# Gated DeltaNet and windowed attention on one core: the merges of the forward and the backward chunk traced in step, their 64x64 products queued in turn

## The chip, the cores and the metric

The program runs on one core of a Trainium2 chip. The metric is the device time of one execution in microseconds (us), as the median of several runs; lower is better. Five engines matter: TensorE (PE; its weight loads are PEld), VectorE (DVE), ScalarE (ACT), GpSimd (POOL), and SyncE (SP), which queues most DMAs. Each engine works through its own queue in the order that was written down when the kernel was built. Line numbers such as L999 are lines of the kernel before.

## The reference: what is computed

One transformer layer over 2048 latent tokens with 256 context tokens in front, model width 1024. Two token mixers run side by side from one input projection:

- A is a bidirectional gated DeltaNet with 4 heads of width 128. It runs over 18 chunks of 128 tokens, once from the front (direction d = 0) and once from the back (d = 1). Inside a chunk the recurrence needs the inverse of a unit triangular matrix of 128x128 for each head; between chunks a 128x128 state of each head is carried on.
- B is windowed attention of 8 query heads over 2 key heads, in blocks of 128 tokens.

Both are gated, projected to width 1024, weighted by sigmoid gates and added, and go through an output projection:

```
y  = sigmoid(ga) * (ya @ w_proj_a) + sigmoid(gb) * (yb @ w_proj_b)
x  = x + gate * (y @ w_out)
```

The inverse in question is `triangular_solve(a_mat, eye)`. A 128x128 triangular matrix with 64x64 diagonal blocks A, B and lower block C has the inverse with blocks A', B' on the diagonal and -B' C A' below, where A', B' are the inverses of the diagonal blocks.

## The kernel before, in words

The program has five parts in time. Up to about 630 us the inputs are normalised and the q, k, v and attention projections are made. From 631 us `gates` makes the 24 row groups of the gate projections in four column groups, 96 tiles in all, by `fm_dense` (L526, L527, L528: one 128x512 product each, 24 products to a tile; their output is called `rps`). VectorE meanwhile inverts the 64x64 diagonal blocks (`base`, L749 and L751; `base4` for the last two chunks, L781 to L793). From about 920 us `scan` runs the two recurrences over 18 steps; then `attention` works through 32 units (a block of 128 queries and one key head); among its later units and after them `project` does the branch projections (L1201 to L1203, output `pps`), and the output projection ends the program.

In a step of the scan each direction has a `chain` (L1055) that carries the state: products `ksps` (L1070), `vps` (L1076) and `sps` (L1088), with VectorE work between them. A `merge` (L969) of each direction makes the whole inverse of the next chunk out of the two 64x64 inverses:

1. two DMAs bring the diagonal blocks into `X` (`mx`), one brings the lower block into `off` (`moff`);
2. TensorE transposes (L988 for d = 0, L990 for d = 1) into the PSUM tile `mtp`;
3. d = 0: ScalarE copies to `W` (L997), four products `myp` (L999), VectorE scales them (L1000), four products `mep` (L1002), ScalarE writes the block (L1003). d = 1: VectorE scales (L1005), four products `myp` (L1007), ScalarE copies (L1008), four products `mep` (L1010), ScalarE writes the block (L1011).

Each of these products is 64 rows by 64 columns in float32, one for each head. The start partition of the operands (0 or 64) picks the half of the rows of PE's 128x128 array, the start partition of the output the half of its columns: so each product works in one quarter of the array. `myp` of d = 0 has rows 64 to 127 and columns 0 to 63, and `myp` of d = 1 has the same quarter. `mep` of d = 0 has rows and columns 0 to 63, `mep` of d = 1 rows 0 to 63 and columns 64 to 127.

The three PSUM tiles of a direction (`mtp`, `myp`, `mep`) take turns in one bank, `mg0` or `mg1`.

The order of the instructions on each engine isn't written by hand. The framework plays the program through a cost model when it is built, and queues what it deems ready, by priority: the scan has high priority, the gate tiles of two column groups (`hh_148` and `hh_150`) fill the gaps that it leaves on TensorE. `tc.issue_after(i)` makes an instruction queue only behind instruction i.

Of the kernel before, what the change touches and what calls it, by code (L numbers as in the profile page):

```python
# [20 lines left out]
H = 4  # L21
# [19 lines left out]
def _hybrid(ctx, tc, nc, V, S, G, T, ins, out, dbg, upto):  # L41
    dma = nc.sync.dma_start
# [17 lines left out]
    ident = cst.tile([128, 128], F32, name="ident")  # L60
# [38 lines left out]
    offsp = [dscr(f"offsp{d}", [NC, 64, H, 64]) for d in range(2)]  # L99
# [3 lines left out]
    Xsp = [{}, {}]  # L103
    X4sp = dscr("X4sp", [2, 2, 4, 8, 64, 16])
# [147 lines left out]
    if True:  # L252
# [48 lines left out]
        for j in range(2):  # L301
            mps = [psum("acc" if n == 0 else "hps", [4, 512], name=f"mps{n}") for n in range(2)]
            for k in range(KT):
# [17 lines left out]
            mtp = psum("kt", [128, 8, 2], name="mtp")  # L321
# [69 lines left out]
        def qk_norm_rope(pool, bufs, ps, nh, c, wn):  # L391
# [28 lines left out]
        def state_pair(c, pss):  # L420
# [64 lines left out]
        for gi in range(8):  # L485
            xts = []
            for j in range(2):
                c = NCB + gi * 2 + j
# [9 lines left out]
            c = NCB + gi * 2  # L498
# [12 lines left out]
    br = pers2.tile([128, NC, 8], F32, name="br")  # L511
# [196 lines left out]
    bs_ = tc.tile_pool(name="base", bufs=1, side="right", reuse_waits="tile")  # L708
# [57 lines left out]
    def base4(fr, bk):  # L766
# [15 lines left out]
        V.tensor_tensor(N[0:32], N[0:32], nb[0:32].unsqueeze(2).to_broadcast(sh), op=ALU.mult)  # L782
        G.memset(X, 0.0)
        for q in range(4):
            if q:
                dma(N[q * 32:q * 32 + 32], N[0:32])
            G.memset(X[q * 32:q * 32 + 32].rearrange("p r s -> p (r s)")[:, 16 * q:16 * q + 976:65], 1.0)
        for m in range(63):
            r, n = 63 - m, m // 4 + 1
            tv = tmp[:, :r * n].rearrange("p (r s) -> p r s", s=n)  # L790
            V.tensor_tensor(tv, N[:, m + 1:, m].unsqueeze(2).to_broadcast([128, r, n]),
                            X[:, m, 0:n].unsqueeze(1).to_broadcast([128, r, n]), op=ALU.mult)
            V.tensor_tensor(X[:, m + 1:, 0:n], X[:, m + 1:, 0:n], tv, op=ALU.add)  # L793
# [47 lines left out]
    LAST = (LAT(14, 15), LAT(0, 1))  # L841
# [35 lines left out]
    def attention(pool, big, blocks, cc):  # L877
        kc, vc, sk, band = cc

        def queries(n):  # L880

            lo_b, hi_b = max(n - 1, 0), min(n + 1, NB - 1)
            nw_ = hi_b - lo_b + 1
            W = nw_ * 128
            t0 = (NCB + lo_b) * 128
# [9 lines left out]
        def scores(n, kv, qq):  # L895
            kw, vw, qT, nw_ = qq
            W = nw_ * 128
            p = big.tile([128, 4, 640], F32, name="pr", bufs=3)
# [67 lines left out]
            weighted(n, kv, qs[n], pr.pop(i))  # L966


    def merge(pool, d, c):  # L969

        X = pool.tile([128, H, 128], F32, name=f"mx{d}", bufs=2)
        G.memset(X, 0.0)
        if c in LAST[d]:
            x4 = pool.tile([128, 4, H, 16], F32, name="x4")
            for b in range(2):
                bs_ = slice(b * 64, b * 64 + 64)
                for q in range(4):
                    dma(x4[bs_, q], X4sp[d, LAST[d].index(c), q, b::2].rearrange("h r s -> r h s"))
                G.tensor_copy(X[bs_, :, bs_].rearrange("p h (s q) -> p h s q", q=4), x4[bs_].rearrange("p q h s -> p h s q"))
        else:  # L980
            for b in range(2):
                dma(X[b * 64:b * 64 + 64, :, b * 64:b * 64 + 64], Xsp[d][c][:, b].rearrange("h r c -> r h c"))
        off = pool.tile([128, H, 64], F32, name=f"moff{d}", bufs=2)
        dma(off[64:128], offsp[d][c])
        tps = psum(f"mg{d}", [128, H, 128], name="mtp")
        for h in range(H):
            if d == 0:
                T.transpose(tps[:, h], X[:, h], ident)  # L988
            else:
                T.transpose(tps[:, h, 64:128], X[64:128, h], ident[64:128, 64:128])  # L990
        brb = br[:, c, d * 4:d * 4 + 4].unsqueeze(2).to_broadcast([128, H, 64])
        y1 = off if d == 0 else pool.tile([128, H, 64], F32, name=f"my{d}")
        yps = psum(f"mg{d}", [128, H, 128], name="myp")
        eps_ = psum(f"mg{d}", [128, H, 128], name="mep")
        if d == 0:
            W = pool.tile([128, H, 128], F32, name="mw", bufs=2)
            S.copy(W, tps)  # L997
            for h in range(H):
                T.matmul(yps[0:64, h, 0:64], lhsT=off[64:128, h], rhs=W[64:128, h, 64:128], start=True, stop=True)  # L999
            V.tensor_tensor(y1[0:64], yps[0:64, :, 0:64], brb[0:64], op=ALU.mult)  # L1000
            for h in range(H):
                T.matmul(eps_[0:64, h, 0:64], lhsT=X[0:64, h, 0:64], rhs=y1[0:64, h], start=True, stop=True)  # L1002
            S.activation(W[0:64, :, 64:128], eps_[0:64, :, 0:64], AF.Copy, scale=-1.0)  # L1003
            return W
        V.tensor_tensor(y1[64:128], tps[64:128, :, 64:128], brb[64:128], op=ALU.mult)  # L1005
        for h in range(H):
            T.matmul(yps[0:64, h, 0:64], lhsT=off[64:128, h], rhs=y1[64:128, h], start=True, stop=True)  # L1007
        S.copy(y1[0:64], yps[0:64, :, 0:64])  # L1008
        for h in range(H):
            T.matmul(eps_[64:128, h, 0:64], lhsT=y1[0:64, h], rhs=X[0:64, h, 0:64], start=True, stop=True)  # L1010
        S.activation(X[64:128, :, 0:64], eps_[64:128, :, 0:64], AF.Copy, scale=-1.0)  # L1011
        return X

    def scan_consts(pool):
        gw = pool.tile([128, 1], F32, name="gw")
# [29 lines left out]
    def scan(pool, pool2, cs):  # L1045

        state = [None, None]
        orders = ([0, 1] + LAT(*range(NB)), [1, 0] + LAT(*range(NB - 1, -1, -1)))
# [50 lines left out]
        def output(d, st, S0, v2):  # L1099
# [26 lines left out]
            else:  # L1126
                dma(osp[b], oa.rearrange("p h d -> p (h d)"))
                seen.add(b)

        W = [merge(pool, d, orders[d][0]) for d in range(2)]  # L1130
        for st in range(NC):
            r = [chain(d, st, W[d]) for d in range(2)]
            ready = [finalize(pool2, b, oa, cs, d) for b, oa, d in late]
            late.clear()
            if st + 1 < NC:
                W = [merge(pool, d, orders[d][st + 1]) for d in range(2)]
            for rest in ready:
                rest()
            for d in range(2):
                if orders[d][st] >= NCB:  # L1140
                    output(d, st, *r[d])
# [3 lines left out]
    with tc.tile_pool(name="scan", bufs=1, side="right", reuse_waits="tile") as scp:  # L1145
        scl_ = tc.tile_pool(name="scan2", bufs=1, reuse_waits="tile")
        scl = scl_.__enter__()
        cs = scan_consts(scl)
# [93 lines left out]
    with tc.tile_pool(name="p4r", bufs=2, side="right", reuse_waits="tile") as pr4, \  # L1242
# [15 lines left out]
        with tc.high_priority(tc.cur_priority - p_last):  # L1258
            yy = load_half(0)
            for k in range(KT):  # L1260
                if k < NWO:
                    pool = pr4 if k < 2 else p4
# [15 lines left out]
        for i, hb in enumerate(halves):  # L1278
# [14 lines left out]
            for tb, n, ps in tiles:  # L1293
                products(tb, n, ps, range(NWO if i == 0 else 0, KT))
                b = hb * 2 + tb
# [56 lines left out]
```

## Time and profile before

| | |
|---|---|
| median of 3 runs | 2039.22 us (2037.51 to 2040.39) |
| the profiled execution, its own time | 2041.74 us |
| span of its trace | 2040.0 us |
| TensorE busy | 1963.6 us, 96% |
| VectorE, ScalarE, GpSimd busy | 1408.4, 786.9, 686.4 us |
| granted TensorE clock, mean | 0.988 |
| first and last product of the merges | 929.1 and 1308.3 us |

The profile lists start and duration of each instruction, and for idle time what ended it. A TensorE record of a matmul lasts longer than the time until the next can start, because they are pipelined; so what a matmul costs TensorE is read from start to start. A float32 product of two float32 operands leaves two records, each with its own weight load: the 72 products of one merge line (18 steps, 4 heads) are 144 records.

### The profile page before, as it was taken

Reading aid. Unit: us, or ns where it says so; the run is one execution under the profiler, and the core shown is the slowest. Engines: PE = TensorE matmul, PEld = TensorE weight load, DVE = VectorE, ACT = ScalarE, POOL = GpSimd, SP = SyncE. Lnnn points to the kernel's source line nnn. Section 1 sums busy time; section 2 is a strip of 40 time slices with the busy share of each in tenths; the row PEclk is TensorE's granted clock in tenths of the full one; section 3 lists DMA queues with packets and bytes.
Section 4 is the critical chain, followed back from the end, with each engine's and each line's share of the span. In section 5 each row is a group of like instructions: output and inputs, shape, how many; then the busy total and the mean of one; then the engine's idle time right before and its main releaser. Section 6 shows DMA issues by size and latency. Waiting matters only on the chain. (4 is left out here: it accounts for less than half of the span.)

```text
span 2040.0 us, 32043 instructions
## 1 busy us (share of the span) xinstructions
PE 1963.6 (96%) x11043; PEld 1641.5 (80%) x11043; DVE 1408.4 (69%) x2715; ACT 786.9 (39%) x1975; POOL 686.4 (34%) x828
## 2 busy tenths in 40 slices
PE   6999999989999899999899999999989999999999
PEld 3888888778898778788788888878868888878887
DVE  6888766667666999999599655636587778743322
ACT  5655555444443322111122222325475556531100
POOL 2862211235652211014222234323256443432321
PEclk7999999999999999999999999999999999999999
DMA  7462236755447533537966788663356655355542
GB/s 254 142 168 81 93 94 166 183 151 158 145 141 195 161 110 112 140 98 222 217 207 205 222 233 226 180 199 123 128 161 204 192 158 169 113 179 180 185 145 93
DMA packets 375510, 333.11 MB, mean 163 GB/s; under 512 B 83832, under 2 KB 299184, under 8 KB 374708
## 3 DMA queue, kind: packets, MB, share of 16 engines
q1 hardware_dynamic: 347924, 288.59, 48.9%
q10 hardware_dynamic: 27424, 42.48, 5.8%
q8 instruction: 87, 1.43, 0.3%
q14 instruction: 75, 0.61, 0.1%
HBM read 220.28 MB, written 109.13 MB: 161 GB/s over the span
## 5 line engine op out<-in xcount | busy, mean ns | idle before, releaser
L526 PE MATMUL rps<-hh,wh 128*128 128x512 f32 x768 | 308.6, 402 | 7.8 <-DVE rt L814 5.6
L528 PE MATMUL rps<-hh,wl 128*128 128x512 f32 x768 | 309.4, 403 | 0.0
L527 PE MATMUL rps<-hl,wh 128*128 128x512 f32 x768 | 307.4, 400 | 0.0
L526 PEld LDWEIGHTS rps<-hh,wh 128*128 128x128 f32 x768 | 145.3, 189 | 43.0 <-DVE rt L814 6.5
L526 PE MATMUL lps<-hh,wh 128*128 128x512 f32 (+1 forms) x448 | 172.1, 384 | 0.3 <-ACT y L636 0.3
L527 PEld LDWEIGHTS rps<-hl,wh 128*128 128x128 f32 x768 | 145.2, 189 | 33.1
L528 PEld LDWEIGHTS rps<-hh,wl 128*128 128x128 f32 x768 | 145.1, 189 | 32.5
L527 PE MATMUL lps<-hl,wh 128*128 128x512 f32 (+1 forms) x448 | 171.1, 382 | 0.0
L528 PE MATMUL lps<-hh,wl 128*128 128x512 f32 (+1 forms) x448 | 171.0, 382 | 0.0
L565 DVE SCALAR_TENSOR_TENSOR cacc<-y,cw,cacc 128x512 f32<-128x512 f32 (+1 forms) x224 | 160.2, 738 | 14.9 <-ACT cacc L563 12.0
L912 DVE CUSTOM_DVE_ANT_0 pr<-sc,band,sk 128x640 f32<-128x640 f32 (+1 forms) x128 | 106.3, 862 | 43.5 <-PE sc L908 22.1
L938 ACT CAST ph<-pt 128x512 fp32r<-128x512 f32 x156 | 90.1, 585 | 111.4 <-PE pt L936 78.9
L940 DVE TENSOR_TENSOR pl<-pt,ph 128x512 fp32r<-128x512 f32 x156 | 104.8, 684 | 39.8 <-ACT ph L938 39.2
L812 ACT ACTIVATE rt<-rps 128x512 f32<-128x512 f32 x96 | 57.2, 596 | 183.2 <-PE rps L528 177.6
L922 POOL TENSOR_SCALAR pr<-pr,sm 128x640 f32<-128x640 f32 (+1 forms) x128 | 98.8, 791 | 56.9 <-DVE sm L920 44.4
L749 DVE TENSOR_TENSOR btmp<-N 128x62 f32<-128x62 f32 (+30 forms) x124 | 115.5, 931 | 3.2
L751 DVE TENSOR_TENSOR N<-N,btmp 128x62 f32<-128x62 f32 (+30 forms) x124 | 114.9, 926 | 3.1
L914 ACT ACTIVATE pr<-pr,sm 128x640 f32<-128x640 f32 (+1 forms) x128 | 104.0, 815 | 24.7 <-DVE sm L912 24.7
L1201 PE MATMUL pps<-yh,wph 128*128 128x512 f32 x256 | 105.5, 416 | 7.2 <-ACT yh L1183 4.1
L245 POOL TENSOR_SCALAR wh<-wr 128x512 fp32r<-128x512 f32 x72 | 48.7, 690 | 172.9 <-PE lps L527 85.3
L246 DVE TENSOR_TENSOR wl<-wr,wh 128x512 fp32r<-128x512 f32 x120 | 91.6, 780 | 20.0 <-POOL wh L245 16.7
L1202 PE MATMUL pps<-yl,wph 128*128 128x512 f32 x256 | 102.2, 399 | 0.5 <-DVE yl L1184 0.5
(302 smaller groups left out, 4950.0 us busy)
## 6 DMA issues: line engine op xcount, KB each, us to landing
wr<-in_w_in_dram SPq DMA_DIRECT2D x120, 256.0 KB
kw<-Ksp SPq DMA_DIRECT2D x28, 384.0 KB
x<-vsp SPq DMA_DIRECT2D x36, 256.0 KB
k<-ksp SPq DMA_DIRECT2D x34, 256.0 KB
kT<-kTsp SPq DMA_DIRECT2D x34, 256.0 KB
wm<-in_w_mod_dram SPq DMA_DIRECT2D x16, 512.0 KB
xt<-in_x_dram SPq DMA_DIRECT2D x16, 512.0 KB
dtl<-Dsp SPq DMA_DIRECT2D x32, 256.0 KB
```

The costliest lines, as they stand in the source:

```text
L526: T.matmul(ps, lhsT=wh[:, k], rhs=xh[:, k], start=k == 0, stop=False)
L527: T.matmul(ps, lhsT=wh[:, k], rhs=xl[:, k], start=False, stop=False)
L528: T.matmul(ps, lhsT=wl[:, k], rhs=xh[:, k], start=False, stop=k == kt - 1)
L565: V.scalar_tensor_tensor(a, y[:, t:t + n], cw[:, m, t:t + 1], a, op0=ALU.mult, op1=ALU.add)
L749: V.tensor_tensor(tv, A[:, m + 1:, m].unsqueeze(2).to_broadcast([h1 + n, r, m]), A[:, m, 0:m].unsqueeze(1).to_broadcast([h1 + n, r, m]), o ...
L751: V.tensor_tensor(A[:, m + 1:, 0:m], A[:, m + 1:, 0:m], tv, op=ALU.add)
L912: V.tensor_tensor_reduce(s_, ps[:, o:768], band[:, b0:b0 + W + 256], -0.125, sk[:, 1, hd:hd + 1], ALU.add, ALU.min, sm[:, h, 1:2])
L914: S.activation(s_, s_, AF.Exp, scale=-1.0, bias=sm[:, h, 1:2], accum_out=sm[:, h, 2:3])
L922: G.tensor_scalar(p[:, h, :W + 256], p[:, h, :W + 256], sm[:, h, 3:4], 1.0, op0=ALU.mult, op1=ALU.mult)
L940: V.tensor_tensor(pl, pt, f32(ph), op=ALU.subtract)
L1201: T.matmul(ps, lhsT=wh[:, k, ms], rhs=hs[k], start=k == 0, stop=False)
L1202: T.matmul(ps, lhsT=wh[:, k, ms], rhs=ls[k], start=False, stop=False)
```

## The change

`merge` now takes both chunks of a step. It loads for both directions first, then transposes for both, then does the two scalings and copies, and then calls `in_step` twice: once for the eight `myp` products, once for the eight `mep` products. `in_step` queues them head by head, forward and backward in turn. The backward `myp` is written to partitions 64 to 127 instead of 0 to 63, which puts it into the quarter with rows and columns 64 to 127; ScalarE's copy behind it reads there and still writes partitions 0 to 63. Sizes, counts of instructions, tiles and PSUM banks are as before.

```diff
-    def merge(pool, d, c):
...
+    def in_step(products):
+        first = None
         for h in range(H):
+            for p in products:
+                with tc.issue_after(first.ins) if first else nullcontext():
+                    i = p(h)
+                first = i
+
+    def merge(pool, cs):
...
+        W, X = pool.tile([128, H, 128], F32, name="mw", bufs=2), Xs[1]
+        S.copy(W, tp[0])
+        V.tensor_tensor(y1[64:128], tp[1][64:128, :, 64:128], brb[1][64:128], op=ALU.mult)
+        yps = [psum(f"mg{d}", [128, H, 128], name="myp") for d in range(2)]
+        in_step([lambda h: T.matmul(yps[0][0:64, h, 0:64], lhsT=offs[0][64:128, h], rhs=W[64:128, h, 64:128],
+                                    start=True, stop=True),
+                 lambda h: T.matmul(yps[1][64:128, h, 0:64], lhsT=offs[1][64:128, h], rhs=y1[64:128, h],
+                                    start=True, stop=True)])
+        V.tensor_tensor(y0[0:64], yps[0][0:64, :, 0:64], brb[0][0:64], op=ALU.mult)
+        S.copy(y1[0:64], yps[1][64:128, :, 0:64])
+        eps_ = [psum(f"mg{d}", [128, H, 128], name="mep") for d in range(2)]
+        in_step([lambda h: T.matmul(eps_[0][0:64, h, 0:64], lhsT=Xs[0][0:64, h, 0:64], rhs=y0[0:64, h],
+                                    start=True, stop=True),
+                 lambda h: T.matmul(eps_[1][64:128, h, 0:64], lhsT=y1[0:64, h], rhs=X[0:64, h, 0:64],
+                                    start=True, stop=True)])
+        S.activation(W[0:64, :, 64:128], eps_[0][0:64, :, 0:64], AF.Copy, scale=-1.0)
+        S.activation(X[64:128, :, 0:64], eps_[1][64:128, :, 0:64], AF.Copy, scale=-1.0)
+        return W, X
...
-        W = [merge(pool, d, orders[d][0]) for d in range(2)]
+        W = merge(pool, [orders[d][0] for d in range(2)])
...
-                W = [merge(pool, d, orders[d][st + 1]) for d in range(2)]
+                W = merge(pool, [orders[d][st + 1] for d in range(2)])
```

In the changed kernel `myp` stands at L1016 and L1018, `mep` at L1023 and L1025; lines behind `merge` are 17 higher.

TensorE at the second merge of the scan, where the forward and the backward `myp` stood apart. Before:

```order
L1088 MATMUL sps<-v_10230,k_10220 128x128 x4
L999 MATMUL myp<-mw,moff_10262 64x64 x4
L1088 MATMUL sps<-v_10249,k_10239 128x128 x4
...
L526 MATMUL rps<-hh_148,wh 128x512
L527 MATMUL rps<-hl_149,wh 128x512
L528 MATMUL rps<-hh_148,wl 128x512
L1007 MATMUL myp<-my_10294,moff_10287 64x64 x4
L528 MATMUL rps<-hh_150,wl 128x512
```

The same place now:

```order
L1016 MATMUL myp<-mw,moff_10262 64x64
L1105 MATMUL sps<-v_10249,k_10239 128x128 x4
L1018 MATMUL myp<-my_10280,moff_10268 64x64
L1016 MATMUL myp<-mw,moff_10262 64x64
L1018 MATMUL myp<-my_10280,moff_10268 64x64
L1016 MATMUL myp<-mw,moff_10262 64x64
L1018 MATMUL myp<-my_10280,moff_10268 64x64
L1016 MATMUL myp<-mw,moff_10262 64x64
L1018 MATMUL myp<-my_10280,moff_10268 64x64
```

Two groups of four have become one group of seven, with one product left alone in front of it. Over the whole scan the products of the merges stand in 78 unbroken groups before and in 53 now; of the 53, 24 hold all eight products, and 11 hold one.

TensorE among the attention units, where the first products of `project` are queued. Before:

```order
L943 MATMUL av<-pl,vc 128x512
L936 MATMUL pt<-ident,pr 128x128 x4
L1201 MATMUL pps<-yh,wph 128x512
L942 MATMUL av<-ph,vc 128x512
L905 MATMUL sc<-kw,qT 128x384
```

Now:

```order
L936 MATMUL pt<-ident,pr 128x128 x4
L1218 MATMUL pps<-yh,wph 128x512
L1219 MATMUL pps<-yl,wph 128x512
L1220 MATMUL pps<-yh,wpl 128x512
L1218 MATMUL pps<-yh,wph 128x512
L1219 MATMUL pps<-yl,wph 128x512
L1220 MATMUL pps<-yh,wpl 128x512
```

These rows follow from a shift ahead of them. Of the 2304 gate products, 1968 stood ahead of the scan's last transposes (L1040) before, and 2064 do now: 96 have moved into the scan. The gate products ended within the seventh unit of the attention, and end within the fifth now; those of `project` began within the tenth, and begin within the ninth now. From the end of the seventeenth unit on the counts of both agree again.

More of the change, by code (lines that the diff above doesn't have):

```diff
@@ L966, in attention @@
             weighted(n, kv, qs[n], pr.pop(i))
-    def merge(pool, d, c):
[L971 to L985, printed above, removed]
-        for h in range(H):
-            if d == 0:
-                T.transpose(tps[:, h], X[:, h], ident)
-            else:
[L990 to L1012, printed above, removed]
@@ new lines, in in_step @@
+    def in_step(products):
+        first = None
+        for h in range(H):
+            for p in products:
[3 more added lines that the diff above has]
+    def merge(pool, cs):
+        hs = range(H)
+        Xs, offs, tp = [], [], []
+        for d, c in enumerate(cs):
+            X = pool.tile([128, H, 128], F32, name=f"mx{d}", bufs=2)
+            G.memset(X, 0.0)
+            if c in LAST[d]:
+                x4 = pool.tile([128, 4, H, 16], F32, name="x4")
+                for b in range(2):
+                    bs_ = slice(b * 64, b * 64 + 64)
+                    for q in range(4):
+                        dma(x4[bs_, q], X4sp[d, LAST[d].index(c), q, b::2].rearrange("h r s -> r h s"))
+                    G.tensor_copy(X[bs_, :, bs_].rearrange("p h (s q) -> p h s q", q=4),
+                                  x4[bs_].rearrange("p q h s -> p h s q"))
+            else:
+                for b in range(2):
+                    dma(X[b * 64:b * 64 + 64, :, b * 64:b * 64 + 64], Xsp[d][c][:, b].rearrange("h r c -> r h c"))
+            off = pool.tile([128, H, 64], F32, name=f"moff{d}", bufs=2)
+            dma(off[64:128], offsp[d][c])
+            Xs.append(X)
+            offs.append(off)
+        for d in range(2):
+            tps = psum(f"mg{d}", [128, H, 128], name="mtp")
+            for h in hs:
+                if d == 0:
+                    T.transpose(tps[:, h], Xs[0][:, h], ident)
+                else:
+                    T.transpose(tps[:, h, 64:128], Xs[1][64:128, h], ident[64:128, 64:128])
+            tp.append(tps)
+        brb = [br[:, c, d * 4:d * 4 + 4].unsqueeze(2).to_broadcast([128, H, 64]) for d, c in enumerate(cs)]
+        y0, y1 = offs[0], pool.tile([128, H, 64], F32, name="my1")
+        W, X = pool.tile([128, H, 128], F32, name="mw", bufs=2), Xs[1]
[16 more added lines that the diff above has]
+        return W, X
```

## The prediction

> **What bounds the kernel now.** I read the page first, for the engine that is full, then the scan's stretch by windows and waits, since all that the change touches lies there.
>
> ```profile
> span 2040.0 us, 32043 instructions
> PE 1963.6 (96%) x11043; PEld 1641.5 (80%) x11043; DVE 1408.4 (69%) x2715; ACT 786.9 (39%) x1975; POOL 686.4 (34%) x828
> 920.00:1357.00 437.00, 426.46 (x2938) 367.42 (x2938) 299.64 (x699) 107.73 (x361) 140.23 (x215) 0.99 0.74 212
> PE aps L1111 <- DVE oa L1123: 5.1, 2, 4.6
> PE ksps L1070 <- DVE S L1094: 2.4, 1, 2.4
> PE rps L526 <- POOL wh L245: 1.2, 1, 1.2
> PE mtp L990 <- ACT mw L997: 0.7, 1, 0.7
> ```
>
> The windows row has PE, PEld, DVE, ACT and POOL in this order, then clock, DMA share and GB/s; the last four rows are the longest waits of TensorE in the same 437 us. TensorE is busy for 426.5 of them and idle for 10.5, and of that idle time only 0.7 us hangs on a merge. So the scan's stretch is bound by TensorE's own sequence: gate products fill whatever the recurrence leaves. What shortens that sequence shortens the stretch, as long as the moved work is covered.
>
> **What the 64x64 products cost TensorE.** Three places of the trace, TensorE in order of time (start, duration, line, operand, shape, count); what counts is start to start.
>
> ```profile
> 928.79 0.40 PE L527 MATMUL rps<-hl,wh 128*128 128x512 f32 x1
> 929.11 0.68 PE L999 MATMUL myp<-mw,moff 64*64 64x64 f32 x8
> 929.63 0.63 PE L1007 MATMUL myp<-my,moff 64*64 64x64 f32 x8
> 930.19 0.49 PE L528 MATMUL rps<-hh,wl 128*128 128x512 f32 x1
> 930.52 0.40 PE L526 MATMUL rps<-hh,wh 128*128 128x512 f32 x1
> 930.75 0.39 PE L527 MATMUL rps<-hl,wh 128*128 128x512 f32 x1
> ...
> 944.27 1.05 PE L1088 MATMUL sps<-v,k 128*128 128x128 f32 x8
> 945.25 0.68 PE L999 MATMUL myp<-mw,moff 64*64 64x64 f32 x8
> 945.86 1.16 PE L1088 MATMUL sps<-v,k 128*128 128x128 f32 x8
> ```
>
> A gate product normally takes 0.23 us to the next (930.52 to 930.75). A group of eight records alone lasts from 945.25 to 945.86, 0.61 us. To it come the way in and out: 928.79 to 929.11 is 0.32 us where 0.23 is normal, 0.09 more, and 930.19 to 930.52 is 0.33, 0.10 more. So a lone group costs 0.61 + 0.09 + 0.10 = 0.80 us. Two groups behind one another in the same quarter, as here, cost 930.52 - 928.79 - 2 x 0.233 = 1.26 us: the second adds only its records, 0.46 us or 0.058 each. A lone group's 0.80 is thus 8 x 0.058 = 0.47 for the records and 0.33 for entering and leaving.
>
> Two groups in different quarters:
>
> ```profile
> 934.72 0.39 PE L526 MATMUL rps<-hh,wh 128*128 128x512 f32 x1
> 935.04 0.50 PE L1002 MATMUL mep<-moff,mx 64*64 64x64 f32 x5
> 935.33 0.27 PE L1010 MATMUL mep<-mx,my 64*64 64x64 f32 x1
> 935.38 0.22 PE L1002 MATMUL mep<-moff,mx 64*64 64x64 f32 x1
> 935.44 0.22 PE L1010 MATMUL mep<-mx,my 64*64 64x64 f32 x1
> 935.44 0.22 PE L1002 MATMUL mep<-moff,mx 64*64 64x64 f32 x1
> ...
> 935.55 0.45 PE L1010 MATMUL mep<-mx,my 64*64 64x64 f32 x5
> 935.93 0.50 PE L527 MATMUL rps<-hl,wh 128*128 128x512 f32 x1
> 936.27 0.39 PE L528 MATMUL rps<-hh,wl 128*128 128x512 f32 x1
> ...
> 1171.17 0.27 PE L1002 MATMUL mep<-moff,mx 64*64 64x64 f32 x1
> 1171.18 0.27 PE L1007 MATMUL myp<-my,moff 64*64 64x64 f32 x1
> 1171.27 0.22 PE L1002 MATMUL mep<-moff,mx 64*64 64x64 f32 x1
> 1171.29 0.22 PE L1007 MATMUL myp<-my,moff 64*64 64x64 f32 x1
> ...
> 1171.40 0.45 PE L1007 MATMUL myp<-my,moff 64*64 64x64 f32 x5
> 1171.79 0.50 PE L527 MATMUL rps<-hl,wh 128*128 128x512 f32 x1
> ```
>
> At 935 us the backward group starts while three records of the forward one are still to come, and then both run at once, each at 0.058 us. The whole pair costs 936.27 - 934.72 - 0.47 = 1.08 us. The second group starts when the first has about four records left. At 1171 us it is tighter: four records of L1002 were the rest of a group, eight of L1007 followed, and the second stream started 0.01 us behind the first; all twelve took 1171.17 to 1171.79, 0.62 us, what eight alone take. So the riders in the other quarter were free. The change queues the two streams two records by two, so that four records of lead always suffice: I take 0.82 us for a full pair.
>
> Here a rule of the Trainium skill speaks against the change. "TensorE: Matmul & The Clock Gate", Part 3, The mechanism, says that weight loads run beside matmuls in flight only where the row group differs, and that matmuls start and end strictly in program order. Both streams of each new pair share their rows (64 to 127 for `myp`, 0 to 63 for `mep`), so by that rule nothing would overlap. The pair at 935 us shares rows 0 to 63 and does overlap, out of program order; so I go by the rows. What it would make of the time is the second rival.
>
> **The change, term by term.** The products: 576 records stand in 78 groups before. 78 x 0.33 = 25.7 us for entering and leaving, 576 x 0.058 = 33.4 us for records, less about 0.18 us (1.26 - 1.08) in each of some 11 groups that overlap already, 2.0 us: 57 us. Now there are 53 groups, 17.5 us; in them the longer of the two streams sums to 312 records, 18.1 us, and the second streams start 0.01 us late, 0.5 us: 36 us. That saves 21 us of TensorE. If no two streams overlapped, it would be 17.5 + 33.4 = 51, and save 6. The transposes of L990 are also 64 rows; they stand in 21 groups before and 18 now, but 7 shared their entry with a merge group and none does now: I cost that at nothing, within 2 us either way.
>
> Gate products that change place: 96 moved from behind the scan into it, 96 x 0.233 = 22.4 us of TensorE. So the scan ends at 22.4 - 21 = 1.4 us later, with the same cover of each step, and the saving shows only where the gate products are now missing, among the attention units.
>
> ```profile
> 1444.00:1481.00 37.00, 37.00 (x197) 31.13 (x197) 20.43 (x44) 18.34 (x40) 8.82 (x10) 1.00 0.35 111
> 1481.00:1540.00 59.00, 50.16 (x262) 38.38 (x261) 48.91 (x100) 43.61 (x94) 34.23 (x34) 0.97 0.55 168
> 1640.00:1700.00 60.00, 60.00 (x327) 50.68 (x326) 42.80 (x90) 30.62 (x66) 26.85 (x29) 1.00 0.46 144
> ...
> 1481.00:1540.00 59.00, 19.60 (x50) 9.13 (x50) 3.13 (x6) 2.91 (x5) 0.97 0.55 168
> 1540.00:1611.00 71.00, 15.80 (x49) 8.59 (x50) 3.27 (x5) 2.34 (x4) 1.00 0.61 195
> 1481.00:1540.00 59.00, 8.38 (x24) 4.06 (x24) 0.67 (x1) 0.97 0.55 168
> 1540.00:1611.00 71.00, 42.56 (x168) 30.62 (x168) 10.25 (x15) 1.00 0.61 195
> 1640.00:1700.00 60.00, 30.31 (x120) 21.65 (x119) 6.82 (x10) 1.00 0.46 144
> ```
>
> Three rows of all instructions, then two of the tile `av` (ten products to a unit), then three of `pps`. Between 1481 and 1540 us there are five units (50 `av`) with hardly any fill, 11.8 us each, and TensorE is not full: this stretch the vector engines set. Between 1540 and 1611 us five units with 168 fillers take 71 us; 168 x 0.233 = 39.1, so a unit's own work is 6.4 us. Between 1640 and 1700 us 120 fillers in 60 us leave TensorE full at 13.0 us a unit. Now the bare stretch is units five to nine instead of seven to eleven: still five units, 59 us. Behind it, units ten to sixteen have about 25 `pps` products each, as at 1640 us: 7 x 13 = 91 us. Units five to sixteen then take 150 us, where they took 167 (1444 to 1611, to the nearest unit); unit seventeen has 12 products fewer, 2.8 us. Together 20 us come back there, of the 22.4 that left.
>
> Sum: + 1.4 us to the scan's end, - 20 after it, is - 18.6, on the profiled 2041.74 us 2023.1. That execution was 2.5 us above the median 2039.22, so for the median **2021 us**, 0.9% faster.
>
> The waits that the change adds: the forward products now wait for the backward's scaling too, and the other way round. The gate products behind them on TensorE would then stand, and behind those the scan. The cover is long:
>
> ```profile
> L1008 ACT COPY my<-myp x18: 350/364/368, 930.3 to 1298.4; 64x256 f32<-64x256 f32 x18
> ```
>
> The first copy ends at 930.7 us, and its products start at 935.33: 4.6 us of other products lie between, and in the new order about as many gate products stand there. I cost the joint wait at nothing; without that cover it would be up to the 1.2 us of the longest wait on GpSimd above, in each of 36 places.
>
> **The rivals.** *The attention keeps part of it.* The five bare units may become six or seven if the first `pps` products wait for their inputs. For: between 1481 and 1540 us each unit took 11.8 us against 6.4 of own work, so a bare unit more costs up to 5.4 us. Against: the new order puts `project` a unit earlier as well. Two units more, 10.8 us: 2032.
>
> *No overlap in turn.* The pairs in the trace came as blocks, none came two by two; if the alternation broke the overlap, 6 us are saved on TensorE instead of 21. The scan then ends 16.4 us later, the attention returns 20: 2039.2 - 3.6 = 2035.6. Against it speak the records at 1171 us, which alternate singly.
>
> *Slower: the joint queueing makes TensorE wait.* Place: the 36 groups at L1016/L1018 and L1023/L1025. It decides from 18.6 / 36 = 0.52 us a group; at 1.2 us each it is 36 x 1.2 - 18.6 = +25, 2064. For: VectorE once held the scan for 4.6 us (L1123 above) with its queue stuck, and a late scaling of one direction now holds both. Against: 0.7 us in all on merge inputs before, and the cover above.
>
> **How the numbers follow.** Forecast 0.62, attention keeps part 0.16, no overlap 0.13, slower 0.09. The forecast's own range is 2012 to 2028: below it, 22.4 us come back whole and the early idle of TensorE shrinks by some of its 10.5 us; above, half of a bare unit and some new waits. With the second case and most of the third the range is 2012 to 2037. What a measurement can tell is 0.2%, 4 us: faster below 2035.1. Forecast and attention case are faster, of the third a sixth: 0.80; same 0.11; slower 0.09.
>
> **What would show it.** Right: `myp` and `mep` groups alternate at about 0.03 us a record, a full pair from entry to exit near 0.82 us; TensorE's time in 64x64 groups falls by about 21 us; the scan ends within 5 us of before; the stretch from the scan's end to the seventeenth unit is about 20 us shorter. Wrong: alternate records at 0.058 us each; waits of TensorE at L1016 to L1025 of more than a few us in sum; a bare attention stretch of seven units.

## The result, and the profile after

The changed kernel takes 2027.62 us (median of 4 runs, 2026.05 to 2031.62) against 2038.64 us for the kernel before on the same chip (4 runs, 2037.51 to 2040.39): a ratio of 0.9950, 95% interval 0.9936 to 0.9964. So it is faster by 0.5%, 11.0 us. The forecast was 2021 us, a gain of 18 to 19 us: the sign is right, the time lies 0.4 us inside the upper end of the forecast's own range (2012 to 2028), and 7 to 8 us of the gain are missing.

The profiled execution of the change took 2031.62 us, the slowest of its four, 10.1 us less than that of before, where the sum had 18.6; so 8.5 us are missing in this pair. The head and the PE row of its page, the windows row of the same 437 us that the prediction showed, and TensorE's longest waits in it:

```profile
span 2029.9 us, 32046 instructions
PE 1946.6 (96%) x11043; PEld 1629.4 (80%) x11043; DVE 1403.5 (69%) x2715; ACT 786.6 (39%) x1975; POOL 686.3 (34%) x828
...
920.00:1357.00 437.00, 423.12 (x2998) 364.06 (x2997) 301.85 (x700) 110.58 (x362) 138.24 (x212) 0.98 0.74 212
```

```profile
PE ksps L1087 <- DVE S L1111: 7.0, 3, 5.6
PE aps L1128 <- DVE oa L1140: 2.5, 1, 2.5
PE sps L1105 <- DVE v L1096: 1.7, 2, 1.4
PE ops L1139 <- DVE oa L1133: 1.7, 1, 1.7
```

TensorE did 60 records more in the stretch (2998 against 2938) and was busy for less of it: it is idle for 13.9 us instead of 10.5, and its mean clock is 0.98 instead of 0.99. No product of the merges (L1016 to L1025) is in the list of TensorE's waits: the joint input wait didn't come. What grew are waits of the recurrence, all on VectorE: S, oa and v.

TensorE's timeline shows one pair in turn, two of its eight doublets and what stands around it:

```profile
935.72 0.39 PE L527 MATMUL rps<-hl,wh 128*128 128x512 f32 x1
936.04 0.27 PE L1023 MATMUL mep<-moff,mx 64*64 64x64 f32 x1
936.05 0.27 PE L1025 MATMUL mep<-mx,my 64*64 64x64 f32 x1
...
936.50 0.22 PE L1023 MATMUL mep<-moff,mx 64*64 64x64 f32 x1
936.51 0.22 PE L1025 MATMUL mep<-mx,my 64*64 64x64 f32 x1
936.65 0.51 PE L528 MATMUL rps<-hh,wl 128*128 128x512 f32 x1
937.00 0.40 PE L526 MATMUL rps<-hh,wh 128*128 128x512 f32 x1
```

The two streams run 0.01 us apart, each at 0.058 us a record. The pair costs 937.00 - 935.72 - 0.47 = 0.81 us; the forecast had 0.82.

The ends of the scan are its first transpose and its last `fps`, here from the views of those two lines, before and after:

```profile
L988 PE MATMUL mtp<-ident,mx x72: 271/273/328, 923.1 to 1297.6; 128*128 128x128 f32 x72
L1040 PE MATMUL fps<-ident,oa x64: 270/273/332, 1191.3 to 1351.5; 128*128 128x128 f32 x64
```

```profile
L1006 PE MATMUL mtp<-ident,mx x72: 270/272/273, 924.3 to 1302.3; 128*128 128x128 f32 x72
L1057 PE MATMUL fps<-ident,oa x64: 270/272/299, 1195.6 to 1361.3; 128*128 128x128 f32 x64
```

The scan took 428.4 us and takes 437.0, so it ends 9.8 us later, not 1.4; 1.2 of that is a later start, whose cause no run here isolates. From its end to the last `pps` the profile before has 506.4 us, now 486.5: 19.9 us come back.

**The scan, term by term.** All tables below are made in the same way, from the records of TensorE between the first `mtp` and the last `fps`: gate products at 0.233 us each; the merges as start-to-start time in their groups with the way in and out; idle time of TensorE as the stretch less its busy time; and the time lost to the clock, as the sum of (1 - granted clock) over windows of 10 us.

| in us | before | change | difference | forecast |
|---|---|---|---|---|
| merges | 57.0 | 36.8 | -20.2 | -21 |
| gate products (775, 871) | 180.6 | 202.9 | +22.4 | +22.4 |
| TensorE idle | 10.2 | 13.9 | +3.7 | 0 |
| lost to the clock | 5.1 | 8.5 | +3.4 | 0 |
| the scan, as measured | 428.4 | 437.0 | +8.6 | +1.4 |

The four terms make +9.3 where +8.6 was measured. The 0.7 us between them is counted twice: a half clock costs nothing while TensorE stands idle, and of the clock's losses 1.45 us in the change and 0.79 before fall into waits.

### The profile page after: what moved, and what is told of

It reads as the page before. It is cut to its first block, busy times and chain, and to the rows that moved or that the text cites. A ratio compares the mean times of both kernels' runs of the same rounds, so it can differ in the third digit from the quotient of the medians.

```text
span 2029.9 us, 32046 instructions
## 1 busy us (share of the span) xinstructions
PE 1946.6 (96%) x11043; PEld 1629.4 (80%) x11043; DVE 1403.5 (69%) x2715; ACT 786.6 (39%) x1975; POOL 686.3 (34%) x828
## 5 line engine op out<-in xcount | busy, mean ns | idle before, releaser
L565 DVE SCALAR_TENSOR_TENSOR cacc<-y,cw,cacc 128x512 f32<-128x512 f32 (+1 forms) x224 | 159.9, 736 | 14.7 <-ACT cacc L563 11.8
```

Of the source, the lines that this page charges most:

```text
L565: V.scalar_tensor_tensor(a, y[:, t:t + n], cw[:, m, t:t + 1], a, op0=ALU.mult, op1=ALU.add)
```

## The experiments

All runs in one table. Ratios are to the kernel before on the same chip, whose median was 2038 to 2042 us; a kernel's runs spread by some 5 us to either side, so the interval is what counts. The last four columns are of the scan, as above.

| kernel | median, us | ratio, 95% interval | gate products | merges | idle | clock |
|---|---|---|---|---|---|---|
| before | 2038.6 | 1 | 775 | 57.0 | 10.2 | 5.1 |
| the change | 2027.6 | 0.9950 (0.9936 to 0.9964) | 871 | 36.8 | 13.9 | 8.5 |
| the change again | 2030.2 | 0.9953 (0.9937 to 0.9968) | 871 | 36.8 | 12.4 | 6.8 |
| in turn, same quarter | 2037.7 | 0.9987 (0.9974 to 1.0000) | 823 | 49.6 | 10.4 | 3.4 |
| blocks, other quarter | 2042.8 | 1.0009 (0.9994 to 1.0024) | 847 | 46.7 | 14.9 | 6.8 |
| before, quarter alone | 2037.8 | 0.9989 (0.9978 to 1.0000) | 823 | 54.0 | 10.5 | 8.5 |
| change, late base4 | 2024.5 | 0.9916 (0.9899 to 0.9934) | 799 | 35.9 | 11.9 | 5.1 |
| before, late base4 | 2035.3 | 0.9969 (0.9956 to 0.9982) | 775 | 56.0 | 6.1 | 1.7 |
| change, base4 traced later | 2025.7 | 0.9937 (0.9916 to 0.9958) | 799 | 31.8 | 16.1 | 6.8 |
| the same, split on ScalarE | 2035.1 | 0.9970 (0.9958 to 0.9981) | 807 | 34.0 | 17.8 | 6.8 |
| before, no base4 | 2030.5 | 0.9949 (0.9929 to 0.9968) | 727 | 53.9 | 4.4 | 3.4 |
| change, no base4 | 2019.7 | 0.9902 (0.9880 to 0.9925) | 751 | 31.5 | 13.2 | 5.1 |
| before, spill queued by ScalarE | 2041.4 | 1.0004 (0.9989 to 1.0019) | 799 | 54.7 | 9.2 | 3.4 |
| change, spill queued by ScalarE | 2036.0 | 0.9985 (0.9968 to 1.0001) | 847 | 36.5 | 14.5 | 10.2 |

Every edit makes the framework plan the whole order anew, so the count of gate products in the scan moves too; that is why the columns are read, not the medians alone. The columns come from one profiled execution of each kernel. The change has two, and they differ by 1.5 us in idle time and 1.7 in the clock, so differences of that size between two kernels say little.

### What is the gain made of: order, quarter, or both

The same turns, but the backward products go to the forward quarter:

```diff
-                 lambda h: T.matmul(yps[1][64:128, h, 0:64], lhsT=offs[1][64:128, h], rhs=y1[64:128, h],
+                 lambda h: T.matmul(yps[1][0:64, h, 0:64], lhsT=offs[1][64:128, h], rhs=y1[64:128, h],
...
-                 lambda h: T.matmul(eps_[1][64:128, h, 0:64], lhsT=y1[0:64, h], rhs=X[0:64, h, 0:64],
+                 lambda h: T.matmul(eps_[1][0:64, h, 0:64], lhsT=y1[0:64, h], rhs=X[0:64, h, 0:64],
```

> The change with one thing undone: the backward products are written to the same quarter of the array as the forward ones (myp rows 64 to 127, mep rows 0 to 63, columns 0 to 63 both), still queued in turn. Theory A (the time is won by streams that overlap): no record overlaps, the eight products of a pair take 16 x 0.058 us; with the 46 groups of the order that results the merges cost TensorE 46 x 0.33 + 576 x 0.058 = 49 us against 36 in the change and 57 before, so the time lies 10 to 13 us above the change, 2037 to 2041, about where before stood. Theory B (the time is won by queueing the merges together, fewer groups and another order): it stays within 4 us of the change, 2024 to 2032.

Blocks of four in different quarters, instead of turns:

```diff
-        for h in range(H):
-            for p in products:
+        for p in products:
+            for h in range(H):
```

> The change with the alternation undone: four forward products, then four backward ones, in the change's quarters. Theory A: the second stream starts when the first has about four records left, a full pair costs 1.08 instead of 0.82 us; with 55 groups the merges cost about 44 us, 8 more than in the change: 2033 to 2037. Theory B: within 4 us of the change, 2024 to 2032.

The kernel before, with only the backward `myp` moved to the other quarter:

```diff
-            T.matmul(yps[0:64, h, 0:64], lhsT=off[64:128, h], rhs=y1[64:128, h], start=True, stop=True)
-        S.copy(y1[0:64], yps[0:64, :, 0:64])
+            T.matmul(yps[64:128, h, 0:64], lhsT=off[64:128, h], rhs=y1[64:128, h], start=True, stop=True)
+        S.copy(y1[0:64], yps[64:128, :, 0:64])
```

> The kernel before with only the quarter changed: the backward myp goes to partitions 64 to 127; the merges are traced one after the other as before. Theory A: the groups stay mostly apart (69 of them), merge cost about 53 us against 57: 4 us less than before at most, 2033 to 2039. Theory B (fewer groups and another order): the same, since little changes in either. It tells whether the quarter alone is worth anything.

TensorE's timeline at the first `myp` pair, in turn in the same quarter:

```profile
932.01 0.40 PE L527 MATMUL rps<-hl,wh 128*128 128x512 f32 x1
932.34 0.33 PE L1016 MATMUL myp<-mw,moff 64*64 64x64 f32 x2
932.51 0.28 PE L1018 MATMUL myp<-my,moff 64*64 64x64 f32 x2
932.62 0.28 PE L1016 MATMUL myp<-mw,moff 64*64 64x64 f32 x2
...
933.75 0.40 PE L526 MATMUL rps<-hh,wh 128*128 128x512 f32 x1
```

And as blocks in different quarters:

```profile
928.12 0.40 PE L527 MATMUL rps<-hl,wh 128*128 128x512 f32 x1
928.45 0.50 PE L1016 MATMUL myp<-mw,moff 64*64 64x64 f32 x5
928.74 0.27 PE L1018 MATMUL myp<-my,moff 64*64 64x64 f32 x1
...
928.96 0.45 PE L1018 MATMUL myp<-my,moff 64*64 64x64 f32 x5
...
929.68 0.39 PE L526 MATMUL rps<-hh,wh 128*128 128x512 f32 x1
```

In the same quarter each group of two records takes 0.115 us and nothing overlaps: 933.75 - 932.01 - 0.47 = 1.27 us a pair. As blocks the second stream starts when the first has three records left: 929.68 - 928.12 - 0.47 = 1.09 us. In turn and in different quarters it is 0.81. Over the scan that makes 49.6, 46.7 and 36.8 us, from 57.0 before; the quarter alone gives 54.0. So neither half of the change does it: of the 20.2 us, 12.8 hang on the other quarter (49.6 to 36.8); the other 7.4 come with the order, which leaves 46 groups with a way in and out in that kernel where 78 were. This split is rough: in the kernel before, the backward `mep` already had a quarter of its own, and the kernel in turn in the same quarter takes that away too. In time the first and the third of these kernels gain 0.1%, which is at the edge of what their intervals tell from nothing, and the blocks gain nothing: TensorE there waited 6.0 us in one piece for a load of the merge, a wait that no other kernel of this group has at that size:

```profile
PE mtp L1008 <- DMA mx<-Xsp: 6.0, 1, 6.0
```

The blocks' time missed both forecasts, which had counted only the merges; in the scan 72 more gate products (16.8 us), 4.7 us more idle time and 1.7 us of clock stand against the 10.3 us saved.

### Is the missing part the step at 993 us

In the change, the longest wait is the state S of the scan's fourth step. VectorE's timeline there, of the change and then of before:

```profile
993.18 4.41 DVE L781 TENSOR_TENSOR N<-N,btmp 32x4096 f32<-32x4096 f32 x1 [11.58 <-DMA N<-Nsp]
997.52 1.52 DVE L246 TENSOR_TENSOR wl<-wr,wh 128x512 fp32r<-128x512 f32 x1
999.07 0.69 DVE L814 SCALAR_TENSOR_TENSOR rt<-rt,rps 128x512 f32<-128x512 f32 x1
999.67 0.82 DVE L246 TENSOR_TENSOR wl<-wr,wh 128x512 fp32r<-128x512 f32 x1
1000.41 2.14 DVE L1111 SCALAR_TENSOR_TENSOR S<-S,tot,sps 128x128 f32<-128x128 f32 x8
```

```profile
994.37 4.41 DVE L781 TENSOR_TENSOR N<-N,btmp 32x4096 f32<-32x4096 f32 x1 [11.16 <-DMA x<-vsp]
998.72 2.14 DVE L1094 SCALAR_TENSOR_TENSOR S<-S,tot,sps 128x128 f32<-128x128 f32 x8
```

S is queued behind a scaling of `base4` that stands for 11 us and a further 4.4, in both kernels; in the change two `wl` and one `rt` came between as well. I queued L781 later (in the change, and further below in the kernel before):

```diff
-        V.tensor_tensor(N[0:32], N[0:32], nc_.unsqueeze(1).to_broadcast(sh), op=ALU.mult)
+        with tc.issue_after(tiles_done[25].ins):
+            V.tensor_tensor(N[0:32], N[0:32], nc_.unsqueeze(1).to_broadcast(sh), op=ALU.mult)
...
-            V.scalar_tensor_tensor(t, t, 1.0, ps, op0=ALU.add, op1=ALU.mult)
+            tiles_done.append(V.scalar_tensor_tensor(t, t, 1.0, ps, op0=ALU.add, op1=ALU.mult))
...
-    base4(*LAST)
...
-        gates(list(range(4)), (1, 0))
+        gates(list(range(6)), (1, 0))
+        base4(*LAST)
...
-        gates(list(range(4, BESIDE)), (1, 0))
+        gates(list(range(6, BESIDE)), (1, 0))
```

> The change, with the scaling that starts the last inversion (L781) queued later on VectorE, behind the evacuation of a later gate tile, so that VectorE's queue no longer stands 11.6 us for the DMA of N while the state update of the scan waits behind it; base4 and two gate row groups are traced ahead of the scan for that. Theory C (the missing 8 us are stalls at that DMA, whose time does not move with TensorE): the 5.6 us wait of ksps on S and the 2.5 us of aps on oa shrink to under 2 us together and the time falls 5 to 8 us below the change, 2019 to 2023. Rival: the wait turns up elsewhere on VectorE's queue and the time stays within 3 us of the change, 2025 to 2030.

> The change itself, unaltered, beside the next three on one chip, so that they are compared with it and not across chips. Expected from its earlier runs: 2024 to 2032, 8 to 14 us under the kernel before.

The second of these is the changed kernel unaltered, on another chip: 0.9953, so the gain of 0.5% stands. The account of its scan stands in kind: merges 36.8 again, and VectorE keeps TensorE waiting for 12.0 us where it was 12.9. It doesn't stand in size: idle time and clock are 3.9 us over before, not 7.1, in a profiled execution 3.7 us shorter than that of the result. The late base4 gave 0.9916, 2024.46 us, between the two expected spans and the best time of a kernel that does all the work. The wait for S is gone, and others stand in its place:

```profile
PE fps L1058 <- DVE oa L1051: 3.3, 4, 1.8
PE ops L1140 <- DVE oa L1137: 3.2, 1, 3.2
PE ops L1140 <- DVE oa L1134: 1.8, 2, 1.7
```

Next `base4` was only traced later; L781 is queued as the planner likes:

```diff
-    base4(*LAST)
...
+        gates(list(range(6)), (1, 0))
+        base4(*LAST)
...
+        gates(list(range(6, BESIDE)), (1, 0))
```

> The change with base4 traced behind the gate row groups 0 to 5 and not ahead of them; nothing is forced on VectorE's queue (L781 stands at the same place as in the change, so the 11.6 us wait on its DMA should stay). The planner's order differs: 41 merge groups instead of 53 (31 of them whole), 24 gate products moved into the scan instead of 96. Theory A (the time follows what the merges cost TensorE): 41 x 0.33 + 0.058 x 288 + 0.5 = 31 us against 36, so 4 to 6 us below the change, 2020 to 2024. Theory C (stalls at the DMA of N set it): the same stall, so within 3 us of the change, 2025 to 2030.

2025.69 us, at the lower edge of the second span: S still kept TensorE for 5.1 us. Then both kernels without `base4`'s loads of N and its steps on VectorE, which takes L781 out of the question:

```diff
-            dma(N[p0:p0 + 16], Nsp[d][c:c + 2].rearrange("c h b r i -> (c h b) r i"))
-        sh = [32, 64, 64]
-        V.tensor_tensor(N[0:32], N[0:32], nc_.unsqueeze(1).to_broadcast(sh), op=ALU.mult)
...
-        for m in range(63):
...
-            V.tensor_tensor(X[:, m + 1:, 0:n], X[:, m + 1:, 0:n], tv, op=ALU.add)
```

> The kernel before without the work of the last inversion: base4 loads no N, does none of its VectorE steps and writes identity blocks, so the output is not the layer's; everything else is kept. Made as the partner of the next one. 20 to 40 us of VectorE work and a DMA wait of 11 us are gone; TensorE is the bound, so only stalls go: 2026 to 2037.

> The change with the same work left out of base4. In these two orders the merges cost 50 us (67 groups) and 31 us (41 groups), 19 apart. Theory C (the missing 8 us are stalls of VectorE's queue behind base4): without it the change is worth nearly all of that, 15 to 19 us under its partner. Rival (they are lost elsewhere: in the attention, or in other waits of the scan): 8 to 13 us under its partner, as in the full kernels.

The two are 10.7 us apart, as far as the originals (11.0), where the first theory wanted 15 to 19. That theory fell: the missing part doesn't hang on `base4`. Without `base4` in VectorE's queue another instruction stands at the head of it at the same place, and S behind that (VectorE's timeline of the change without `base4`):

```profile
996.13 1.69 DVE L246 TENSOR_TENSOR wl<-wr,wh 128x512 fp32r<-128x512 f32 x2 [10.29 <-POOL wh L245]
997.74 2.15 DVE L1099 SCALAR_TENSOR_TENSOR S<-S,tot,sps 128x128 f32<-128x128 f32 x8
```

### Is it the transfers, or GpSimd in front of VectorE

GpSimd's `wh` in that row stands behind the scaling of `x`, and `x` waits for its load. In the change the load is queued behind a spill of 2 x 1024 KB. I let ScalarE queue the spill, in both kernels, and took the kernel before with the late base4 beside them:

```diff
-            dma(Xset[d][si].rearrange("c h b r j -> (c h b) (r j)"), N[p0:p0 + n].rearrange("p r j -> p (r j)"))
+            (adma if si else dma)(Xset[d][si].rearrange("c h b r j -> (c h b) (r j)"), N[p0:p0 + n].rearrange("p r j -> p (r j)"))
```

> The changed kernel, but the second spill of the finished 64x64 inverses (two transfers of 1024 KB, L761) is queued by ScalarE instead of SyncE. In the changed kernel those two stand at 972.6 us in SyncE's queue, and the x of the scan's fourth step, queued behind them at 986.3, lands at about 993 us; the state S of that step is 5.6 us late for ksps. Theory (the transfers of that step land late, and what TensorE saved in the first steps is waited away there): with the spill in another queue that x starts on GpSimd below 990 us, the wait of ksps for S falls below 2 us, and the scan without its gate products (230 to 234 us in the changed kernel) falls to 227 to 230; 2021 to 2026 us. Rival (the 16 DMA engines are full there, at 0.92 busy, whatever queue asks): x still starts at 992 to 996, the wait stays at 4 to 7 us, 2026 to 2032 us. Gate products queued in the scan: 2040 instead of 2064, 5.6 us less in the scan, which the attention gets.

> The same move of the spill in the kernel before. Theory: its wait of ksps for S in that step is only 2.4 us, so there is less to win: the scan without its gate products goes from 247.6 us to 245 to 248, 2035 to 2040 us; so the difference between this kernel and the changed one with the same move grows from 11 us to 13 to 16. Rival: nothing moves in either, the difference stays at 9 to 12.

> The kernel before, with the late queueing of L781 that took the changed kernel from 0.995 to 0.992 of the time before (base4 traced behind six column groups, its first scaling queued behind the 26th gate tile). Theory (the change overtook the transfers, so the step at 993 us costs the changed kernel more than the kernel before): worth 0 to 2.4 us here, 2036 to 2039 us, with the same 1968 gate products. Rival (the late base4 is worth the same to both): 3 to 6 us, 2033 to 2036.

GpSimd's timeline in the change, and in the change with the spill in the other queue:

```profile
993.81 6.13 POOL L1080 TENSOR_TENSOR x<-x,rin 128x512 f32<-128x512 f32 x2 [8.37 <-DMA x<-vsp]
```

```profile
996.04 6.33 POOL L1080 TENSOR_TENSOR x<-x,rin 128x512 f32<-128x512 f32 x2 [7.36 <-DMA x<-vsp]
```

The `x` starts at 996.0 us instead of 993.8, 1.5 us earlier only if each is counted from the start of its scan, and TensorE's wait for S stays (7.0 us in sum, the longest 4.5). So the place in SyncE's queue isn't what holds it. The time missed both spans: 2036.0 us, with the clock's losses at 10.2 us, the most of all kernels, and a scan that starts 3.7 us later. The kernel before with the same move took 2041.4 us, above its span of 2035 to 2040; so the two are 5.4 us apart here, which misses the 13 to 16 of the theory and the 9 to 12 of its rival. The late base4 in the kernel before took it to 0.9969: it is worth as much there (0.3%) as in the change; idle time and clock together fall by 7.5 us there and by 5.4 in the change. The theory that the change alone ran into fixed landing times falls with that.

Last, the copy into `wh` of the scan's gate tiles by ScalarE instead of GpSimd, on the kernel with base4 traced later:

```diff
-        gates(list(range(6)), (1, 0))
+        gates(list(range(6)), (1, 0), by_act=True)
...
-        gates(list(range(6, BESIDE)), (1, 0))
+        gates(list(range(6, BESIDE)), (1, 0), by_act=True)
```

> The changed kernel with base4 traced later (the run of that name: ratio 0.9937, scan without its gate products 232.0 us, TensorE waiting 15.0 us on VectorE in the scan, VectorE idle 19.2 us there with wl at the head of its queue, which waits for GpSimd's wh), and the copy into wh for the gate tiles of the scan made by ScalarE instead of GpSimd. The same 1992 gate products are queued in the scan. Theory (TensorE time saved in the scan comes back as waits on VectorE, since VectorE's queue stands behind instructions that wait for GpSimd): VectorE's idle time ahead of wl falls below 8 us, TensorE's waits on VectorE to 6 to 10, the scan without gate products to 224 to 228 us, 2018 to 2022 us, a ratio of 0.989 to 0.992. Rival (the recurrence itself is that long, and another wait takes the place): TensorE's waits on VectorE stay at 11 to 15 us, 2023 to 2028 us, 0.992 to 0.995.

VectorE's idle time ahead of `wl` falls from 19.2 to 8.3 us, as meant; TensorE's waits on VectorE do not fall (15.0 us before this edit, 15.3 with it). VectorE now waits longer for another product of GpSimd: 39.6 us for `fss`, where it was 27.7. TensorE's longest waits in it:

```profile
PE ops L1138 <- DVE oa L1132: 5.0, 3, 3.5
PE fps L1056 <- DVE oa L1049: 4.5, 2, 3.6
PE ksps L1086 <- DVE S L1110: 4.1, 1, 4.1
```

The rival was right about the waits, and the time of 2035.1 us is beyond both spans: the scan is 6.2 us longer than without the edit, and what follows it up to the last `pps` 5.6 us longer.

### What the four pairs say together

Each pair is a kernel without and with the change, the rest alike (for the first pair, as profiled for the result):

| pair | merges | idle | clock | medians |
|---|---|---|---|---|
| as they are | -20.2 | +3.7 | +3.4 | -11.0 |
| late base4 | -20.1 | +5.8 | +3.4 | -10.8 |
| no base4 | -22.4 | +8.8 | +1.7 | -10.7 |
| spill queued by ScalarE | -18.2 | +5.3 | +6.8 | -5.4 |

The saving on TensorE is there each time, and each time 7 to 12 us come back as more idle time and a lower clock (3.9 with the second profile of the change); the gate products that move into the scan (24 to 96) are missing behind it. With those at 0.233 us each the terms make +9.3, -5.3, -6.3 and +5.1 us, and the scans moved by +8.6, -2.0, -7.5 and +3.2; so for the late base4 3.3 us stay unexplained.

The idle time that comes is a wait on VectorE: 7.7 to 12.9 us, 5.3 to 9.6, 0.6 to 12.6, and 8.0 to 12.2. The three kernels that save 3 to 10 us on the merges (the quarter alone, in turn in the same quarter, the blocks) have 7.7, 5.0 and 7.1 us of it, no more than before. So it comes with the large savings.

Why it comes is argued, not shown, and there are two readings. The first is a scan whose other half, the recurrence through VectorE with its loads and GpSimd's scalings, did not get shorter along with TensorE's. The second is the order, which is fixed when the kernel is built. In the change TensorE waits 1.67 us for oa up to 1179.92 us. The last `wl` ahead of this wait, and TensorE's last gate product before it and first behind it:

```profile
1163.58 0.67 DVE L246 TENSOR_TENSOR wl<-wr,wh 128x512 fp32r<-128x512 f32 x1
...
1176.04 0.39 PE L527 MATMUL rps<-hl,wh 128*128 128x512 f32 x1
...
1182.33 0.79 PE L528 MATMUL rps<-hh,wl 128*128 128x512 f32 x1
```

The product at 1182.33 us goes on with the tile that stood open at 1176.04, and its weights were made by 1164.25. So TensorE had work there, queued behind the wait; and 240 gate products are still done after the scan. No run here queues such a product earlier. Which link would have to be shortened, or moved, stays open: after each of the three edits (L781 queued later, the spill moved, `wh` made by ScalarE) TensorE still waited on VectorE.

## Why the prediction was right, and where it fell short

**What a pair costs** was right: 0.81 us for 0.82, the merges 20.2 us shorter for 21. The trace of before had the overlap in a few places, and the records there said what the turns would do.

**The rule of the Trainium skill** that I set against it ("TensorE: Matmul & The Clock Gate", Part 3, The mechanism) doesn't describe these products. The records in turn overlap fully although their rows are the same. What decides is the quarter: same rows and same columns, 0.115 us for each two records; same rows and other columns, both streams at full rate. The rival built on it, no overlap in turn, fell; its price can be seen in the kernel with the same quarter, where the merges cost 49.6 us (forecast 51), and 2037.7 us are measured (forecast 2035.6).

**The gate products** came as the order had shown them: 96 more in the scan, 22.4 us.

**The attention** gave back 19.9 us up to the last `pps`, for 20, but in another shape. The windows of `av`, then of `pps`:

```profile
1454.00:1511.00 57.00, 19.81 (x50) 9.05 (x51) 3.38 (x5) 2.92 (x5) 0.97 0.52 158
1511.00:1606.00 95.00, 24.02 (x71) 12.37 (x71) 4.75 (x7) 4.08 (x7) 0.98 0.59 185
1454.00:1511.00 57.00, 6.13 (x22) 4.38 (x22) 0.67 (x1) 0.97 0.52 158
1511.00:1606.00 95.00, 43.94 (x171) 31.31 (x170) 10.22 (x15) 0.98 0.59 185
```

Units five to nine took 57 us for 59 and already carry 22 `pps`; the next seven took 95 for 91. The bare stretch is four units of 10.0 us each, not five of 11.8, so the rival with six or seven bare units fell. Up to unit seventeen 17.2 us came back, and 2.7 us behind it, where the forecast had nothing: that the total agrees so well is in part luck.

**The step that failed** is the sum for the scan: "So the scan ends at 22.4 - 21 = 1.4 us later, with the same cover of each step". The cover wasn't the same. TensorE's idle time there grew by 3.7 us and the clock took 3.4 more; with the start 1.2 us later the scan ended 9.8 us later, against the prediction's own sign, "within 5 us of before". The range had left room above the forecast for "some new waits", without a size. I had treated a stretch in which TensorE is 97.6% busy as bound by TensorE alone, and so the saving as whole. The 10.5 us of idle time in the windows row were the warning: waits of the recurrence, for oa and S, already kept TensorE idle in three places. That a saving on TensorE brings such waits nearer is the reading above, not a result.

**The slower rival** had its place wrong and its worry half right. No wait of the merges' products for their joint inputs is listed in the change; the cover of 4.6 us held. But the other piece that spoke for it, VectorE's queue that once held the scan for 4.6 us, is the kind of wait that grew.

## What to carry to other kernels

Small products of two independent chains, queued in turn in different quarters of the array, cost TensorE what one chain costs (0.81 us a pair, 0.80 a lone group); order or quarter alone gives little, so measure the pair start to start. Where a chain over several engines runs beside the busiest engine and already makes it wait in places, count only part of a saving on that engine (here 11.0 us came of the 18.6 summed): look for those waits, and for a longer one add the clock that it may cost. Moving one blocker out of a queue shows what stands behind it, not that the chain got shorter.

## What was not expected of the hardware

A wait of TensorE can be paid twice. During and behind the 5.56 us for S, and again behind one of 1.67 us, the records of the change run at half rate: the clock is at 0.50 for 10.24 us from 998.85 us on (7.5 of them after the wait), and for 6.83 us from 1179.75 on. TensorE's timeline at the second, and the windows of both:

```profile
1179.92 2.07 PE L1139 MATMUL ops<-v,qd 128*128 128x128 f32 x8 [1.67 <-DVE oa L1133]
...
1182.92 0.63 PE L526 MATMUL rps<-hh,wh 128*128 128x512 f32 x1
1183.35 0.63 PE L527 MATMUL rps<-hl,wh 128*128 128x512 f32 x1
```

```profile
1002.00:1009.00 7.00, 7.00 (x38) 6.14 (x38) 7.00 (x10) 0.76 (x2) 0.53 (x1) 0.50 0.42 112
1179.00:1186.00 7.00, 6.08 (x21) 5.16 (x22) 3.51 (x11) 3.08 (x13) 2.40 (x3) 0.55 0.63 201
```

Between 1002 and 1009 us the granted clock is 0.50 throughout. In the second stretch a gate product takes 0.43 us to the next (1182.92 to 1183.35) instead of 0.233. Not every wait is followed by it: the one of 2.5 us for oa, later in the same scan, isn't. In the scans of these fourteen profiles the clock stands at 0.50 for 3.41 us, or for two or three times that, and the losses are 1.7, 3.4, 5.1, 6.8, 8.5 and 10.2 us, whole multiples of 1.7. The Trainium skill states a rule for this that I hadn't weighed ("TensorE: Matmul & The Clock Gate", Part 1): the clock is halved or full for windows of about 3.4 us, by how busy the array was. By that figure a window at half clock costs 1.7 us, an estimate, and the trace agrees. The Trainium skill asks there for an idle window of about 3.4 us before the clock is halved; that doesn't agree with the 1.67 us here, as TensorE was busy for all of 1173.0 to 1178.2 us, up to this wait.
